# Stick-breaking attention: work taken off GpSimd, and the sum over later key blocks taken as separate products

## The chip, the cores and the metric

The kernel runs on one core of a Trainium2 chip. The metric is the device time of one execution in microseconds, the median of several runs. The engines are named as the profile names them: PE is TensorE (its weight loads are PEld), DVE is VectorE, ACT is ScalarE, POOL is GpSimd, SP is SyncE. Each engine takes its instructions in the order in which the program holds them.

## The reference

A trunk of two layers over 528 tokens (16 meta tokens and 512 real ones) of width 1024: layer 0 mixes tokens by stick-breaking attention with 16 heads of 64, layer 1 by a gated recurrence; a squared-ReLU MLP of width 4096 follows each. The change lies in the attention:

```python
def _sb_block(q_blk, k, v, q_pos):
    t_len = k.shape[2]
    k_pos = jnp.arange(t_len)
    z = jnp.einsum('bhqd,bhkd->bhqk', q_blk, k).astype(jnp.float32) * (SB_HEAD_DIM ** -0.5)
    causal = k_pos[None, :] < q_pos[:, None]
    log_keep = jnp.where(causal, -jax.nn.softplus(z), 0.0)
    after = lax.cumsum(log_keep, axis=3, reverse=True) - log_keep
    w = jnp.where(causal, jnp.exp(jax.nn.log_sigmoid(z) + after), 0.0)
    return jnp.einsum('bhqk,bhkd->bhqd', w.astype(v.dtype), v)
...
        h = h + stick_breaking_mixer(hn, sb_w_qkv[j], sb_w_o[j])
...
        h = h + sq_relu_mlp(hn, mlp_w_up[i], mlp_w_down[i])
```

So a weight needs, for its query, the softplus of all later keys up to that query: a sum that runs backwards over the keys.

## The kernel before

Every float32 operand of a product is written as two halves, a rounded one and the rest (`split`, lines 56 to 61: ACT or DVE makes the rounded half `hi`, line 58 or 60, and DVE or POOL subtracts it, line 61), and a product of two numbers is three matmuls. `load_unit` (line 88) loads 128 x 1024 weights and splits them into `whi` and `wlo`; `v_load` does the same for the weights of v.

The work goes by pairs of heads (`heads`, eight calls, p from 0 to 7), and while a pair is worked on, PE also makes the queries, keys and values of the next (`make_qk`, `make_v`), and behind the last pair the output projection (`proj`, weights `wo`). Within a pair there are two heads (e) and four blocks t of 128 keys. Keys lie on the partitions, and queries along the free dimension, so block t has 288, 272, 400 or 512 columns for t of 3, 2, 1, 0. The blocks go from the last to the first, both heads each time. For each block:

- `do_z`: PE writes scores and mask into the PSUM tile z (four such tiles);
- `do_soft` (lines 411 to 419): three ACT activations and one DVE instruction make softplus in `sp`, and DVE splits it into `sh` (line 60) and `sl` (line 61);
- `do_s` (lines 421 to 442): PE subtracts from z the sums within the block (the triangle `ntri` times sh and sl), and for blocks 2, 1 and 0 the sum over the later blocks, by products with `nones`, a matrix of -1. Block 2 takes sh and sl of block 3 as they are. For blocks 1 and 0, DVE has added softplus of the later blocks column by column into `sp` (lines 434 and 442); this running sum is split anew into `rh` and `rl` (line 438), and these are what `nones` multiplies;
- `do_o`: ACT takes exp of z, the weights are split into `wh` and `wl` (line 448; for blocks 3, 2, 1 by ACT and POOL, for block 0 by DVE), and PE multiplies with v.

POOL also makes the lower halves of the key weights (line 288), of half of the v weights (line 340), of wo (lines 563 and 585), of two half units at the start (line 217), and a small addition per head (line 478). The order on each engine is set by a scheduler, which places instructions by its own estimate of their durations; `tc.high_priority` moves some forward. An engine waits on semaphores for what it reads and for buffers to come free; temporary tiles have rings: 7 for sp, 4 each for sh and sl, 2 each for rh and rl.

Of the kernel before, what the change touches and what calls it, by code (L numbers as in the profile page):

```python
# [16 lines left out]
ALU = mybir.AluOpType  # L17
# [3 lines left out]
KC = 8  # L21
NM = 16
S = 512
T = NM + S
# [13 lines left out]
W3, W2, W1 = 320, 272, 400  # L38
# [3 lines left out]
def tile_hybrid_trunk(ctx: ExitStack, tc: tile.TileContext, h0, vec, wqk, wv, wo, wob,  # L42
# [13 lines left out]
    def split(src, hi, lo, hi_eng=None, lo_eng=None):  # L56
        if hi_eng is None or hi_eng is act:
            act.activation(out=hi, in_=src, func=AF.Copy)  # L58
        else:
            hi_eng.tensor_copy(out=hi, in_=src)  # L60
        (lo_eng or dve).tensor_tensor(out=lo, in0=src, in1=f32(hi), op=ALU.subtract)  # L61
# [26 lines left out]
    def load_unit(src, lo_eng=None, hi_eng=None):  # L88
        with tc.high_priority(HP):
            raw = wp.tile([P, KC * P], F32, tag="raw", name="raw", bufs=3)  # L90
            nc.sync.dma_start(out=raw, in_=src)
            hi = wp.tile([P, KC * P], F32R, tag="whi", name="whi")
            lo = wp.tile([P, KC * P], F32R, tag="wlo", name="wlo")
            split(raw, hi, lo, hi_eng, lo_eng)
        return hi, lo
# [73 lines left out]
    def attention_layer():  # L169
# [11 lines left out]
        def tmp(tag, bufs, dtype=F32):  # L181
            return ap_.tile([P, S], dtype, tag=tag, name=tag, bufs=bufs)
# [8 lines left out]
        def first_half(i, a, lo_eng=None):  # L191
            m, raw, hi, lo = w_first[i]
            half = slice(a * 4 * P, (a + 1) * 4 * P)
            nc.sync.dma_start(out=raw[:, half], in_=wqk[m][:, half])
            split(raw[:, half], hi[:, half], lo[:, half], None, lo_eng)
# [14 lines left out]
        for c in range(KC):  # L210
            if c % 4 == 0:
                hs[c // 4] = hsp.tile([P, 4, TX], F32, tag="hs", name="hs")
                first_half(0, c // 4)
            nc.sync.dma_start(out=h_chunk(c), in_=h0[:, c, :])
            xs_write(c, h_chunk(c), V_MIX0, 0, TX)
            if c % 4 == 3:
                first_half(1, c // 4, pool)
        for c in range(KC):
            first_add(c)
        dve.tensor_tensor(out=nrm.acc, in0=nrm.acc, in1=acc2[:, 0, :], op=ALU.add)  # L220
# [11 lines left out]
            pool.affine_select(out=t, in_=t, pattern=[[step, t.shape[1]]], base=base,  # L232
                               channel_multiplier=mult, compare_op=op, fill=fill)

        scr = tmp("sp", 7)
        t_ = scr[:, 0:P]
        pool.memset(t_, 1.0)
        aff(t_, 0, 1, -1, ALU.is_equal, 0.0)
# [7 lines left out]
        pool.memset(t_, 0.0)  # L246
        aff(t_, NM, -1, 1, ALU.is_gt, NEG)
        pool.tensor_copy(out=m0, in_=t_)
        scr = tmp("sp", 7)
        t_ = scr[:, 0:W2]  # L250
        pool.memset(t_, 0.0)
        aff(t_, 0, -1, 1, ALU.is_gt, NEG)
        pool.tensor_copy(out=m2, in_=t_)
        scr = tmp("sp", 7)
        pool.memset(scr[:, 0:W3], 0.0)
        aff(scr[:, 0:256], -112, -1, 1, ALU.is_gt, NEG)
        aff(scr[:, 256:272], 112, -1, 1, ALU.is_gt, NEG)
# [27 lines left out]
        o = ap_.tile([P, KC, T], F32, name="o")  # L285

        def qk_mm(m, new):
            hi, lo = load_unit(wqk[m], lo_eng=dve if m < KC else pool)
            gs = []
            for c0, n in ALL:  # L290
                g = new()
                gemm([g[:, 0:n]], [(c0, n)],
                     [(hi[:, k * P:(k + 1) * P], lo[:, k * P:(k + 1) * P], xh[k], xl[k]) for k in range(KC)])
                gs.append(g)
            return gs
# [37 lines left out]
        def v_load(g, lo_eng=None):  # L333
            vhi = hsp.tile([P, KC, 256], F32R, tag="hs", name="vhi")
            vlo = hsp.tile([P, KC, 256], F32R, tag="hs", name="vlo")
            for j in range(2):
                raw = wp.tile([P, KC * P], F32, tag="raw", name="raw", bufs=3)
                nc.sync.dma_start(out=raw, in_=wv[g, j])
                r3 = raw.rearrange("p (k n) -> p k n", n=256)
                split(r3, vhi[:, 4 * j:4 * j + 4, :], vlo[:, 4 * j:4 * j + 4, :], lo_eng=lo_eng or (pool, dve)[j])  # L340
            return vhi, vlo

        def v_mm(pv, w, vhi, vlo):
# [27 lines left out]
        def heads(p, q, kk, v2):  # L371
# [34 lines left out]
            def two(src, w, htag, ltag, bufs, hi_eng, lo_eng):  # L406
                h_, l_ = tmp(htag, bufs, F32R), tmp(ltag, bufs, F32R)
                split(src[:, 0:w], h_[:, 0:w], l_[:, 0:w], hi_eng, lo_eng)
                return h_, l_

            def do_soft(t, e):
                w, zt = width[t], z[t, e]
                a = sp[t, e] = tmp("sp", 7)
                act.activation(out=a[:, 0:w], in_=zt[:, 0:w], func=AF.Abs)  # L414
                table(out=a[:, 0:w], in_=a[:, 0:w], func=AF.Exp, tset=LNEXP, scale=-1.0)
                table(out=a[:, 0:w], in_=a[:, 0:w], func=AF.Ln, tset=LNEXP, bias=1.0)
                dve.scalar_tensor_tensor(out=a[:, 0:w], in0=zt[:, 0:w], scalar=0.0, in1=a[:, 0:w],  # L417
                                         op0=ALU.max, op1=ALU.add)
                sh[t, e], sl[t, e] = two(a, w, "sh", "sl", 4, dve, dve)

            def do_s(t, e):
                w, zt = width[t], z[t, e]
                for x in (sh[t, e], sl[t, e]):
                    mm(zt[:, 0:w], ntri, x[:, 0:w], False, False)
                if t == 3:
                    mm(zt[:, 240:256], ones, sp[t, e][:, 272:288], False, False)
                    a, h_, l_ = (x[3, e][:, 240:256] for x in (sp, sh, sl))
                    dve.tensor_tensor(out=a, in0=a, in1=sp[3, e][:, 272:288], op=ALU.add)
                    split(a, h_, l_, dve, dve)
                elif t == 2:  # L430
                    for x in (sh[3, e], sl[3, e]):
                        mm(zt[:, 16:W2], nones, x[:, 0:256], False, False)
                    r, r3 = sp[2, e], sp[3, e]
                    dve.tensor_tensor(out=r[:, 16:W2], in0=r[:, 16:W2], in1=r3[:, 0:256], op=ALU.add)
                else:
                    c = 128 if t == 1 else 112
                    wr = width[t + 1]
                    for x in two(sp[t + 1, e], wr, "rh", "rl", 2, dve if t else act, dve):
                        mm(zt[:, c:c + wr], nones, x[:, 0:wr], False, False)
                    if t == 1:  # L440
                        r = sp[1, e]
                        dve.tensor_tensor(out=r[:, 128:W1], in0=r[:, 128:W1], in1=sp[2, e][:, 0:W2], op=ALU.add)

            def do_o(t, e):
                w, zt = width[t], z[t, e]
                x = tmp("x", 2)
                table(out=x[:, 0:w], in_=zt[:, 0:w], func=AF.Exp, tset=LNEXP)
                ws = two(x, w, "wh", "wl", 2, act if t else dve, pool if t else dve)
                if t == 3:
                    for i, x in enumerate(ws):  # L450
                        mm(po[e][:, 256:512], vst(3, e), x[:, 0:256], i == 0, False)
                    for x in ws:
                        mm(zt[:, 288:320], vst(4, e), x[:, 256:288], False, False)
                    own, oth = sides[e]
                    m = ap_.tile([P, 2 * NM], F32, tag="om", name="om", bufs=2)
                    act.activation(out=m[own, :], in_=zt[oth, 288:320], func=AF.Copy)
                    dve.tensor_tensor(out=ends(o[own, p, :], NM), in0=zt[own, 288:320].rearrange("p (a b) -> p a b", a=2),
                                      in1=m[own, :].rearrange("p (a b) -> p a b", a=2), op=ALU.add)
                else:
                    c = {2: 240, 1: 112, 0: 0}[t]  # L460
                    for x in ws:
                        mm(po[e][:, c:c + w], vst(t, e), x[:, 0:w], False, False)
# [10 lines left out]
            for a, b in ((0, S),) if p < KC - 1 else ((0, HT - NM), (HT - NM, S)):  # L473
                for e, (own, oth) in enumerate(sides):
                    m = tmp("x", 2)
                    act.activation(out=m[own, a:b], in_=po[e][oth, a:b], func=AF.Copy)
                    if b == S:
                        pool.tensor_tensor(out=m[own, S - NM:], in0=o[own, p, T - NM:], in1=m[own, S - NM:], op=ALU.add)
                    dve.tensor_tensor(out=o[own, p, NM + a:NM + b], in0=po[e][own, a:b], in1=m[own, a:b], op=ALU.add)  # L479

        def decay():
# [78 lines left out]
            return xr  # L560

        for m in range(NA):
            proj(m, [(k, k) for k in range(6)], residual(m), load_unit(wo[m], lo_eng=pool))
        o_split(6)
        o_split(7, ALL)
        raw = wp.tile([P, KC * P], F32, tag="raw", name="raw", bufs=3)
# [14 lines left out]
        for m in (4, 5, 0, 1, 6, 2, 3, 7):  # L581
            if m < NA:
                proj(m, [(2 * m, 6), (2 * m + 1, 7)], h_chunk(m), wl_)
            else:
                proj(m, [(k, k) for k in range(8)], residual(m), load_unit(wo[m], lo_eng=pool), ztile)
            final(m)
        xs["h"], xs["l"] = xh, xl
        return nrm
# [316 lines left out]
```

## Time and profile before

| | |
|---|---|
| median of 3 runs | 1246.43 us (1243.47 to 1246.81) |
| the profiled execution | 1246.97 us; its span, from first to last instruction, 1245.1 us |
| PE busy | 1203.9 us, 97% of the span |
| DVE busy | 703.7 us, 57% |
| ACT busy | 562.1 us, 45% |
| POOL busy | 120.3 us, 10% |
| mean granted clock of PE | 0.989 |

The attention, with its output projection, takes about the first 345 us; the first MLP follows. Shares of the whole span are a mean over stages with different limits, so the stretch in which the change lies has to be read by itself. The profile's "busy" of PE counts a matmul from its start to its modelled end, and matmuls overlap, so PE can seem busy across a short pause. Granted clock 1.00 is the full 2.4 GHz; 0.5 would be 1.2 GHz.

### The profile page before, as it was taken

To read this page: it belongs to the slowest core of one execution; us is meant where nothing else is said; L and a number is where in the kernel's file an instruction comes from. 1 tells how busy PE (TensorE), PEld (TensorE's weight loads), DVE (VectorE), ACT (ScalarE), POOL (GpSimd) and SP (SyncE) were. 2 spreads that over 40 slices of the span, in tenths; PEclk is the share of its full clock that TensorE was granted. 3 is DMA by queue.
4 is the path that set the end of the run, shared out by engine and by line. 5 is a ranking of instruction groups with operands and counts; after the bars stand their busy time and mean duration, and the time that the engine had idled before them with its cause. 6 is when DMAs were issued, how large, how long until landed. Compare 5 with 4: busy or idle time off the path is not lost.

```text
span 1245.1 us, 19073 instructions
## 1 busy us (share of the span) xinstructions
PE 1203.9 (97%) x7836; PEld 1103.7 (89%) x7836; DVE 703.7 (57%) x1117; ACT 562.1 (45%) x943; POOL 120.3 (10%) x117
## 2 busy tenths in 40 slices
PE   7999999989999999999999999999999999999997
PEld 6999999878999999999999999777888888888886
DVE  6898989898654422244433377686644233444333
ACT  5777777776443321133322348664433221333321
POOL 5232332344100000000000000000000000000000
PEclk8999999998999999999999999999999999999998
DMA  6221303023222222322222331223233232332322
GB/s 209 81 92 35 90 32 104 18 84 106 69 83 88 85 97 74 102 94 94 85 92 79 102 119 54 83 85 102 87 100 102 85 102 87 100 101 85 102 85 68
DMA packets 33334, 110.13 MB, mean 88 GB/s; under 512 B 3936, under 2 KB 5984, under 8 KB 33248
## 3 DMA queue, kind: packets, MB, share of 16 engines
q1 hardware_dynamic: 32816, 108.53, 26.9%
q8 instruction: 61, 1.00, 0.3%
q10 hardware_dynamic: 432, 0.39, 0.1%
q14 instruction: 25, 0.20, 0.1%
HBM read 102.49 MB, written 2.10 MB: 84 GB/s over the span
## 4 chain that ended last, share of the span: by engine, by line
PE 77%; DVE 13%; ACT 6%; issue 3%; DMA 1%; POOL 0%; SPq 0%; DVEq 0%; ACTq 0%; POOLq 0%
PE g L98 72%; PE z L98 5%; DVE sl L61 2%; PE o L98 1%; DVE sh L60 1%; ACT sp L79 1%; ACT whi L58 1%; DVE k L322 1%; DVE wlo L61 1%; DVE sp L417 1%; DVE o L479 1%; ACT sp L414 1%; DVE th L723 1%; DVE rl L61 1%; DVE q L313 1%
## 5 line engine op out<-in xcount | busy, mean ns | idle before, releaser
L58 ACT ACTIVATE whi<-raw 128x1024 fp32r<-128x1024 f32 (+1 forms) x178 | 186.6, 1050 | 541.7 <-PE g L98 286.9
L61 DVE TENSOR_TENSOR wlo<-raw,whi 128x1024 fp32r<-128x1024 f32 (+1 forms) x161 | 196.7, 1222 | 253.2 <-PE g L98 131.7
L98 PE MATMUL g<-xl,whi 128*128 128x264 f32 (+1 forms) x720 | 231.9, 335 | 0.7 <-DVE xl L61 0.5
L98 PE MATMUL g<-xh,whi 128*128 128x264 f32 (+1 forms) x720 | 232.0, 336 | 0.1
L98 PE MATMUL g<-hh,whi 128*128 128x264 f32 (+2 forms) x784 | 229.3, 318 | 0.0
L98 PE MATMUL g<-hl,whi 128*128 128x264 f32 (+2 forms) x784 | 229.2, 318 | 0.0
L98 PE MATMUL g<-xh,wlo 128*128 128x264 f32 (+1 forms) x720 | 157.5, 335 | 0.8 <-DVE wlo L61 0.8
L98 PEld LDWEIGHTS g<-hl,whi 128*128 128x128 f32 x784 | 147.5, 188 | 11.2
L98 PEld LDWEIGHTS g<-hh,whi 128*128 128x128 f32 x784 | 147.6, 188 | 10.8
L98 PEld LDWEIGHTS g<-xl,whi 128*128 128x128 f32 x720 | 136.3, 189 | 15.8 <-DVE xl L61 1.6
L98 PEld LDWEIGHTS g<-xh,whi 128*128 128x128 f32 x720 | 136.3, 189 | 14.8 <-ACT r L79 0.3
L613 DVE SCALAR_TENSOR_TENSOR t<-g,rstd 128x264 f32<-128x264 f32 (+1 forms) x96 | 46.8, 516 | 172.4 <-PE g L98 172.3
L98 PE MATMUL g<-x,whi 128*128 128x264 f32 x1024 | 137.5, 284 | 1.8 <-DVE hs L553 1.8
L98 PE MATMUL g<-hh,wlo 128*128 128x264 f32 (+2 forms) x784 | 136.7, 319 | 0.0
L98 PEld LDWEIGHTS g<-x,whi 128*128 128x128 f32 x1024 | 130.7, 188 | 2.1 <-ACT whi L58 2.0
L98 PEld LDWEIGHTS g<-xh,wlo 128*128 128x128 f32 x720 | 118.7, 189 | 14.9 <-DVE wlo L61 1.1
L98 PEld LDWEIGHTS g<-hh,wlo 128*128 128x128 f32 x784 | 115.5, 188 | 10.8
L98 PE MATMUL g<-x,wlo 128*128 128x264 f32 x512 | 78.3, 285 | 0.0
L98 PEld LDWEIGHTS g<-x,wlo 128*128 128x128 f32 x512 | 69.2, 188 | 0.1
L79 ACT ACTIVATE sp<-sp 128x400 f32<-128x400 f32 (+3 forms) x128 | 62.0, 510 | 1.1
L61 POOL TENSOR_TENSOR wl<-x,wh 128x288 fp32r<-128x288 f32 (+2 forms) x48 | 53.1, 1113 | 70.6 <-ACT wh L58 48.1
L797 POOL MEMSET identf<- 128x128 f32 x1 | 0.2, 205 | 544.0 <-PE g L98 544.0
(201 smaller groups left out, 1779.6 us busy)
## 6 DMA issues: line engine op xcount, KB each, us to landing
raw<-in_wup_dram SPq DMA_DIRECT2D x64, 512.0 KB, 3.2
raw<-in_wdn_dram SPq DMA_DIRECT2D x64, 512.0 KB, 3.2
raw<-in_win_dram SPq DMA_DIRECT2D x16, 512.0 KB, 3.3
raw<-in_wqk_dram SPq DMA_DIRECT2D x14, 512.0 KB, 3.3
q<-q SPq DMA_DIRECT2D x16, 264.0 KB, 3.7
raw<-in_wv_dram SPq DMA_DIRECT2D x8, 512.0 KB, 3.3
raw<-in_wo_dram SPq DMA_DIRECT2D x8, 512.0 KB, 3.4
raw<-in_wout_dram SPq DMA_DIRECT2D x8, 512.0 KB, 3.3
```

Source lines behind the costliest of these rows:

```text
L58: act.activation(out=hi, in_=src, func=AF.Copy)
L60: hi_eng.tensor_copy(out=hi, in_=src)
L61: (lo_eng or dve).tensor_tensor(out=lo, in0=src, in1=f32(hi), op=ALU.subtract)
L79: ins = act.activation(out=out, in_=in_, func=func, **kw)
L98: return pe.matmul(out=o, lhsT=lhsT, rhs=rhs, start=start, stop=stop, skip_group_check=True)
L313: dve.tensor_tensor(out=q[own, e, 1, :], in0=t[own, 0:T], in1=f32(q[own, e, 0, :]), op=ALU.subtract)
L322: dve.tensor_tensor(out=kk[oth, e, :], in0=t[own, :], in1=f32(kk[own, e, :]), op=ALU.subtract)
L414: act.activation(out=a[:, 0:w], in_=zt[:, 0:w], func=AF.Abs)
L417: dve.scalar_tensor_tensor(out=a[:, 0:w], in0=zt[:, 0:w], scalar=0.0, in1=a[:, 0:w], op0=ALU.max, op1=ALU.add)
L479: dve.tensor_tensor(out=o[own, p, NM + a:NM + b], in0=po[e][own, a:b], in1=m[own, a:b], op=ALU.add)
L613: dve.scalar_tensor_tensor(out=t3[:, i, :], in0=g[:, i, 0:cw], scalar=0.0, in1=r3[:, i, :], op0=ALU.max, op1=ALU.mult)
L723: dve.tensor_tensor_scan(out=ths[n], data0=rs[n], data1=is_[n], initial=0.0, op0=ALU.mult, op1=ALU.add)
```

## The change

Block t now multiplies `nones` with the halves sh and sl of each later block by itself, so for block 1 four products and for block 0 six, where each had two. The running sum is gone: the two DVE additions and the splits into rh and rl. The halves of all four blocks have to live until block 0 is done, so their rings grow from 4 to 7, and that of sp shrinks to 5. Everything that POOL split or added in this stage is done by DVE. The masks and constants that POOL makes at the start, its three multiplications and additions for the first norm, and its few instructions at the very end of the program stay.

```diff
@@ first units, key weights, v weights
-                first_half(1, c // 4, pool)
+                first_half(1, c // 4)
...
-            hi, lo = load_unit(wqk[m], lo_eng=dve if m < KC else pool)
+            hi, lo = load_unit(wqk[m], lo_eng=dve)
...
-                split(r3, vhi[:, 4 * j:4 * j + 4, :], vlo[:, 4 * j:4 * j + 4, :], lo_eng=lo_eng or (pool, dve)[j])
+                split(r3, vhi[:, 4 * j:4 * j + 4, :], vlo[:, 4 * j:4 * j + 4, :], lo_eng=dve)
@@ do_soft, do_s, do_o
-                a = sp[t, e] = tmp("sp", 7)
+                a = sp[t, e] = tmp("sp", 5)
...
-                sh[t, e], sl[t, e] = two(a, w, "sh", "sl", 4, dve, dve)
+                sh[t, e], sl[t, e] = two(a, w, "sh", "sl", 7, dve, dve)
...
-                elif t == 2:
-                    for x in (sh[3, e], sl[3, e]):
-                        mm(zt[:, 16:W2], nones, x[:, 0:256], False, False)
-                    r, r3 = sp[2, e], sp[3, e]
-                    dve.tensor_tensor(out=r[:, 16:W2], in0=r[:, 16:W2], in1=r3[:, 0:256], op=ALU.add)
-                else:
-                    c = 128 if t == 1 else 112
-                    wr = width[t + 1]
-                    for x in two(sp[t + 1, e], wr, "rh", "rl", 2, dve if t else act, dve):
+                first = (NM, 128, 256, 272)
+                for t2 in range(t + 1, 4):
+                    c, wr = first[t2] - first[t], 256 if t2 == 3 else width[t2]
+                    for x in (sh[t2, e], sl[t2, e]):
                         mm(zt[:, c:c + wr], nones, x[:, 0:wr], False, False)
-                    if t == 1:
-                        r = sp[1, e]
-                        dve.tensor_tensor(out=r[:, 128:W1], in0=r[:, 128:W1], in1=sp[2, e][:, 0:W2], op=ALU.add)
...
-                ws = two(x, w, "wh", "wl", 2, act if t else dve, pool if t else dve)
+                ws = two(x, w, "wh", "wl", 2, act if t else dve, dve)
...
-                        pool.tensor_tensor(out=m[own, S - NM:], in0=o[own, p, T - NM:], in1=m[own, S - NM:], op=ALU.add)
+                        dve.tensor_tensor(out=m[own, S - NM:], in0=o[own, p, T - NM:], in1=m[own, S - NM:], op=ALU.add)
@@ output projection, twice
-            proj(m, [(k, k) for k in range(6)], residual(m), load_unit(wo[m], lo_eng=pool))
+            proj(m, [(k, k) for k in range(6)], residual(m), load_unit(wo[m]))
```

The scheduler reorders with it. The first place is DVE at the end of the third pair of heads, before. sp_1614 and sp_1639 are softplus of block 0 of the two heads, sp_1825 is block 3 of the next pair.

```order
L417 SCALAR_TENSOR_TENSOR sp_1639<-z_1558,sp_1639 128x512 [waits Activation_49]
L61 TENSOR_TENSOR rl_1651<-sp_1588,rh_1650 128x400 [waits Activation_49]
L61 TENSOR_TENSOR sl_1620<-sp_1614,sh_1619 128x512 [waits DVE_49]
L60 CAST sh_1644<-sp_1639 128x512 [waits DVE_49]
L302 SCALAR_TENSOR_TENSOR qk32_2107<-g_2082,rstd_437 128x264 [waits PE_49]
L61 TENSOR_TENSOR wlo_2622<-raw_2619,whi_2621 128x1024 [waits DMAHW1_49,Activation_49]
L61 TENSOR_TENSOR sl_1645<-sp_1639,sh_1644 128x512 [waits DVE_49]
L313 TENSOR_TENSOR q_2110<-qk32_2107,q_2110 64x528 [waits DMAHW6_49,DMAHW5_49,Activation_49]
L313 TENSOR_TENSOR q_2110<-qk32_2107,q_2110 64x528 [waits Activation_49]
L417 SCALAR_TENSOR_TENSOR sp_1825<-z_1805,sp_1825 128x288 [waits PE_49,Activation_49]
L60 CAST wh_1633<-x_1631 128x512 [waits Activation_49]
```

The same place in the changed kernel (block 0 is sp_1590 and sp_1615, the next pair's block 3 is sp_1801):

```order
L60 CAST sh_1595<-sp_1590 128x512 [waits DVE_49]
L417 SCALAR_TENSOR_TENSOR sp_1615<-z_1540,sp_1615 128x512 [waits Activation_49]
L61 TENSOR_TENSOR sl_1596<-sp_1590,sh_1595 128x512 [waits DVE_49]
L302 SCALAR_TENSOR_TENSOR qk32_2075<-g_2050,rstd_437 128x264 [waits PE_49]
L61 TENSOR_TENSOR wlo_2582<-raw_2579,whi_2581 128x1024 [waits DMAHW1_49,Activation_49]
L417 SCALAR_TENSOR_TENSOR sp_1801<-z_1781,sp_1801 128x288 [waits Activation_49]
L313 TENSOR_TENSOR q_2078<-qk32_2075,q_2078 64x528 [waits DMAHW6_49,DMAHW5_49,Activation_49]
L60 CAST sh_1620<-sp_1615 128x512 [waits PE_49]
L313 TENSOR_TENSOR q_2078<-qk32_2075,q_2078 64x528 [waits Activation_49]
L61 TENSOR_TENSOR sl_1621<-sp_1615,sh_1620 128x512 [waits DVE_49,PE_49]
L61 TENSOR_TENSOR wl_1585<-x_1582,wh_1584 128x400 [waits Activation_49]
L60 CAST sh_1806<-sp_1801 128x288 [waits PE_49]
```

rl is gone and a wl that POOL had made stands among the rows. The cast of the second head's block 0 (sh_1620), and that of the next pair's block 3 (sh_1806), now wait for PE: with rings of seven, the eighth tile takes the place of one that the products of block 0 read last. Between sl_1621 and sh_1806 stands one wl of 400 columns.

The second place is PE, block 0 of the first head of the same pair, before:

```order
L98 MATMUL o0_1424<-wl_1583,v2_1278 128x400 [waits Pool_49]
L98 MATMUL z_1532<-sl_1620,ntri_176 128x512 [waits DVE_49]
L98 MATMUL z_1532<-rh_1625,nones_177 128x400
L98 MATMUL z_1532<-rl_1626,nones_177 128x400
L98 MATMUL z_1558<-sh_1644,ntri_176 128x512 [waits DVE_49]
```

and in the changed kernel, as far as the next row of the projection (g):

```order
L98 MATMUL z_1515<-sl_1596,ntri_176 128x512 [waits DVE_49]
L98 MATMUL z_1515<-sh_1549,nones_177 128x400
L98 MATMUL z_1515<-sl_1550,nones_177 128x400
L98 MATMUL z_1515<-sh_1499,nones_177 128x272
L98 MATMUL z_1515<-sl_1500,nones_177 128x272
L98 MATMUL z_1515<-sh_1435,nones_177 128x256
L98 MATMUL z_1515<-sl_1436,nones_177 128x256
L98 MATMUL g_2091<-xh5_77,wlo_2088 128x264
```

Six products with nones follow the triangle where there were two, and none of the six has a wait of its own.

## Rows read from the trace of the kernel before

**Rows 1.** Windows (us): busy PE, PEld, DVE, ACT, POOL (count), granted clock, DMA

```profile
25.00:275.00 250.00, 237.36 (x1773) 227.52 (x1772) 226.15 (x479) 186.98 (x417) 83.34 (x67) 1.00 0.23 70
275.00:300.00 25.00, 25.00 (x168) 24.43 (x169) 18.97 (x45) 16.22 (x37) 8.89 (x8) 0.87 0.29 88
300.00:325.00 25.00, 21.55 (x128) 19.68 (x127) 16.31 (x27) 10.21 (x21) 5.30 (x5) 0.86 0.22 73
375.00:400.00 25.00, 25.00 (x207) 25.00 (x207) 11.86 (x19) 10.16 (x15) 0.00 (x0) 1.00 0.26 85
```

**Rows 2.** Waits on PE, 25 to 345 us: us in total, times, longest us

```profile
PE z L98 <- DVE sl L61: 4.9, 4, 2.0
PE z L98 <- DVE k L322: 3.7, 2, 3.4
PE z L98 <- DVE sh L60: 3.2, 5, 1.3
```

**Rows 3.** Groups by form, 0 to 480 us: busy us, mean ns, idle before

```profile
L60 DVE CAST sh<-sp 128x16 fp32r<-128x16 f32 x16 | 8.7, 542 | 0.2 <-PE z L98 0.2
L60 DVE CAST sh<-sp 128x512 fp32r<-128x512 f32 x16 | 11.3, 709 | 0.0
L60 DVE CAST wh<-x 128x512 fp32r<-128x512 f32 x16 | 6.7, 422 | 5.7 <-ACT x L79 5.5
L61 DVE TENSOR_TENSOR sl<-sp,sh 128x512 fp32r<-128x512 f32 x16 | 15.5, 975 | 0.1
L61 DVE TENSOR_TENSOR wl<-x,wh 128x512 fp32r<-128x512 f32 x16 | 11.0, 687 | 1.2 <-PE o L98 0.5
L322 DVE TENSOR_TENSOR k<-qk,k 64x544 fp32r<-64x544 f32 x16 | 16.0, 1001 | 1.5 <-ACT k L321 1.0
```

**Rows 4.** Tiles sh and k on DVE: ns min/median/max, first and last start

```profile
L60 DVE CAST sh<-sp x80: 156/358/2498, 44.8 to 309.4; 128x288 fp32r<-128x288 f32 x16, 128x16 fp32r<-128x16 f32 x16, 128x272 fp32r<-128x272 f32 x16, 128x400 fp32r<-128x400 f32 x16
L322 DVE TENSOR_TENSOR k<-qk,k x16: 718/721/2746, 37.9 to 276.0; 64x544 fp32r<-64x544 f32 x16
```

**Rows 5.** Timelines of DVE, POOL and PE near 275 and 306 us: start, us

```profile
272.18 2.75 DVE L322 TENSOR_TENSOR k<-qk,k 64x544 fp32r<-64x544 f32 x1
271.68 2.67 POOL L61 TENSOR_TENSOR wlo<-raw,whi 128x1024 fp32r<-128x1024 f32 x1
274.98 1.03 PE L98 MATMUL z<-q,k 128*128 128x256 f32 x4 [3.42 <-DVE k L322]
277.76 0.42 PE L98 MATMUL g<-xh,whi 128*128 128x264 f32 x1
277.98 0.42 PE L98 MATMUL g<-xl,whi 128*128 128x264 f32 x1
305.87 0.70 PE L98 MATMUL z<-sl,ntri 128*128 128x400 f32 x1 [2.04 <-DVE sl L61]
```

**Rows 6.** Work that goes: tile rl (ns min/median/max), then groups by form

```profile
L61 DVE TENSOR_TENSOR rl<-sp,rh x32: 423/561/2012, 54.2 to 309.0; 128x272 fp32r<-128x272 f32 x16, 128x400 fp32r<-128x400 f32 x16
L60 DVE CAST rh<-sp 128x272 fp32r<-128x272 f32 x16 | 6.7, 418 | 0.2
L434 DVE TENSOR_TENSOR sp<-sp 128x256 f32<-128x256 f32 x16 | 8.2, 512 | 0.1
L442 DVE TENSOR_TENSOR sp<-sp 128x272 f32<-128x272 f32 x16 | 6.9, 435 | 0.1
```

**Rows 7.** Groups by form, 0 to 480 us: DVE prices for moved work

```profile
L61 DVE TENSOR_TENSOR wlo<-raw,whi 128x1024 fp32r<-128x1024 f32 x31 | 37.9, 1222 | 32.9 <-PE g L98 23.2 <-ACT whi L58 9.7
L61 DVE TENSOR_TENSOR sl<-sp,sh 128x288 fp32r<-128x288 f32 x16 | 7.2, 453 | 0.2
```

**Rows 8.** Timeline of PE: start, us, of products that follow each other

```profile
296.82 0.52 PE L98 MATMUL z<-q,k 128*128 128x400 f32 x2
297.18 0.28 PE L98 MATMUL z<-m,ident 128*128 128x256 f32 x1
297.30 0.29 PE L98 MATMUL o<-wl,v 128*128 128x272 f32 x1
```

More of the change, by code (lines that the diff above doesn't have):

```diff
@@ L233, in aff @@
                                channel_multiplier=mult, compare_op=op, fill=fill)
-        scr = tmp("sp", 7)
+        scr = tmp("sp", 5)
         t_ = scr[:, 0:P]
@@ L248, in attention_layer @@
         pool.tensor_copy(out=m0, in_=t_)
-        scr = tmp("sp", 7)
+        scr = tmp("sp", 5)
         t_ = scr[:, 0:W2]
@@ L253, in attention_layer @@
         pool.tensor_copy(out=m2, in_=t_)
-        scr = tmp("sp", 7)
+        scr = tmp("sp", 5)
         pool.memset(scr[:, 0:W3], 0.0)
@@ L584, in attention_layer @@
             else:
-                proj(m, [(k, k) for k in range(8)], residual(m), load_unit(wo[m], lo_eng=pool), ztile)
+                proj(m, [(k, k) for k in range(8)], residual(m), load_unit(wo[m]), ztile)
             final(m)
```

## Prediction

> **What bounds the kernel now.** I read the windows first, since the change touches only the first 345 us. In the stretch from 25 to 275 us, which holds nearly all of the heads, PE is busy 237 of 250 us and DVE 226 of 250, so 90% [rows 1]. Two in-order engines are both nearly full, and each waits for the other at times. In the pure matmul stretch at 375 us, PE does 207 products of 264 columns in 25 us, one per 0.121 us, and is never idle [rows 1]. That pace tells more than "busy". In the heads' stretch stand 1773 products. At 0.121 us each they need 214.5 us. The wide ones cost more: two of 400 columns take 0.36 us together, so 0.18 each, while products of 256 and 272 columns follow each other at 0.12 [rows 8]; in proportion 512 columns cost 0.23. A head has eight of 400 and six of 512, and the stretch holds about 14 heads: 14 x (8 x 0.06 + 6 x 0.11) = 16 us. Six narrow ones per head, taken at nothing, take 10 us off. That leaves 220 of 250 us; some records can be missing, so I put PE's lost time there at 25 us.
>
> Who ends it shows in the list of waits on PE: DVE's sl, k and sh, 11.8 us together [rows 2]. These are plain short instructions, so the next question is why they come late. The groups by form answer it. Casting 128x512 costs DVE 709 ns for sh and 422 for wh; the subtraction of the same shape costs 975 for sl and 687 for wl; a cast of 16 columns costs 542 [rows 3], though the shortest sh takes 156; k takes 1001 on average, but 718 at least and 2746 at most [rows 3, 4]. So some executions are stretched severalfold. The timeline shows one: POOL's wlo runs from 271.68 for 2.67 us; DVE's k begins in it, at 272.18, and ends 0.6 us after it; PE waits 3.42 us for k, and then issues products every 0.22 us instead of 0.12 [rows 5]: it has fallen from its 2.4 GHz level to 1.2. The granted clock is 0.87 and 0.86 in the two windows from 275 to 325 us [rows 1]; in the second, too, a wait for DVE stands, 2.04 us for sl at 305.87 [rows 5]. The Trainium skill (SBUF — State Buffer, "Who interferes with whom") has a rule for this: GpSimd and DVE share one pair of ports, and the later of the two is blocked for the whole instruction of the other. By it k would last 274.35 - 272.18 + 0.72 = 2.89 us; the trace says 2.75, so it agrees.
>
> **The change, part by part.**
>
> *PE gains work.* Block 1 has two more products of 256 columns, block 0 two of 272 and two of 256: six per head, 96 in 16 heads, at 0.12 us [rows 8]: **+11.6 us**. PE is the engine that is nearly full and nothing covers this, except time in which PE would have waited anyway.
>
> *DVE loses work.* Per head the two additions (512 and 435 ns), the cast to rh (418) and two subtractions to rl (561 at the median) go: 2.49 us, times 16, 39.8 us [rows 6]. ACT loses the other cast to rh.
>
> *DVE gains POOL's work.* 7 key units, 8 units of wo and 3 of v at 1.22 us make 22.0; two half units some 1.3; wl of 288 columns at 0.45, of 272 at no more than that, and of 400 at 0.57 (between 453 ns for 288 and 687 for 512), 16 times each, 23.5; 16 additions on 16 columns at 0.16, 2.6 [rows 3, 4, 7]. Together +49.4 us.
>
> *DVE is no longer stretched.* From four forms alone, 16 of each: (542 - 156) + (709 - 422) + (975 - 687) + (1001 - 718) ns, times 16, is 19.9 us [rows 3, 4]; other forms come on top. So DVE ends with 49.4 - 39.8 - 19.9, **10 us less work** or better, although it took over what POOL did. Bounds: 10 us more, if the stretching has another cause; 30 less, if all other forms together gain as much again as these four. None of this is on the path by itself. It counts where PE waits for DVE.
>
> *PE's lost time in the heads.* Of 25 us I let half go: **-12.5**. That is the listed waits for the three DVE results, without the 2.04 at 306 (9.8 us, [rows 2, 5]), and a small part of the short ones that no row names. Bounds: only the wait for k goes (-3.4); all 25 go. I take the middle because the stretched forms are just those named in the waits, while the new order brings waits of its own.
>
> *PE's lost time in the tail.* The clock: 25 x 0.13 + 25 x 0.14 = 6.75 us in two windows [rows 1]; with the wait at 306, **-8.8**. PE sat idle before both falls, in waits for k and for sl. If neither wait is there, I expect the clock to stay up. Bounds: 0 (another wait takes their place) and -8.8.
>
> *The start.* Two half units move from POOL to DVE, while POOL's multiplications for the norm stay and go on colliding. 1.3 us more on DVE, less stretching: 0, within 1.5 either way.
>
> *Rings.* Softplus halves now live through the whole pair, and the casts of the second head's block 0 and of the next pair's block 3 wait for PE to read the tile whose place they take. What stands behind them on DVE is wl and wh for block 0 and evictions of the next projection. Eight products of block 0 last 2 x (0.23 + 0.18 + 0.12 + 0.12) = 1.3 us; the wl between takes 0.57, so such a cast can wait 0.7 us and more. I take 0 for it, since DVE has room for it now; its upper bound is in the rivals. Buffers of sp (5 in place of 7) cost nothing, as sp is done once its halves exist.
>
> *Sum:* 11.6 - 12.5 - 8.8 = -9.7 us. From the profiled 1246.97 that gives 1237.3; the median of the runs shown is 0.5 us lower, so I predict **1236.7 us**. (No change means within 0.3%, or 3.7 us: about what a measurement of this kernel can tell.)
>
> **Rivals.**
>
> *Deep gain.* All of PE's lost time goes, 25 in the heads and 8.8 in the tail: 11.6 - 33.8 = -22, about 1224 us. For it: DVE has more room everywhere, and the chain between blocks is shorter, because block 0 needs no addition, cast and subtraction on the way. Against it: short waits arise in any such interleaving.
>
> *A wash.* The gain is only the wait for k and the tail, 12.2 us, and the 96 products take back 11.6: 1246 us. For it: PE was 95% busy in the heads, and work added to a full engine is certain, while work off its partner is not.
>
> *Slower, by the rings.* Two casts per pair wait for PE up to 1.3 us each, 15 of them in eight pairs, and all that DVE owes PE stands behind them: 15 x 1.3 = 20 us handed on to PE, so 1236.7 + 20 = 1257. It decides the sign from 9.7 / 15 = 0.65 us per wait that reaches PE. Against it: products of the next projection lie between, which PE does meanwhile.
>
> *Slower, by load.* If the stretching isn't POOL's doing, DVE, at 90% before, gets 49.4 - 39.8 = 10 us more and hands it on to PE, which has 11.6 more of its own: up to 1268 if both add, 1257 if one hides the other. The rows speak against it, as above. The Trainium skill (Perfetto Trace Analysis, "Optimizing Scalar/DVE Operations") has a rule against this change: work of a saturated DVE may go to another engine, even GpSimd. It adds that between these two it might not help, for the shared port; rows 5 bear out the addition.
>
> *The change is not what it says.* POOL keeps the masks, the norm and the end, all outside the heads, so in the heads it really is idle; I give this no chance.
>
> **How the numbers follow.** Forecast (-4 to -17 us) 0.61, deep gain 0.16, wash 0.13, slower by the rings 0.06, by load 0.04. Faster by over 0.3% are the first two, 0.77; same 0.13; slower 0.10. The range runs from 1222, just beyond the deep gain's middle, to 1249, which takes in the wash with room for 2 or 3 us of the new waits; outside it I leave about 0.07 below and 0.12 above.
>
> **What would show it.** POOL has no row between 25 and 345 us. Mean durations of sh, sl and k are at their free values: 512 columns at 0.42 and 0.69, k at 0.72. DVE's busy time from 25 to 345 us falls by at least 10 us. 96 more products with nones. The granted clock stays near 1.00 around 300 us. DVE waits for PE before a cast to sh, 15 or so times. The first MLP begins about 10 us earlier. I am wrong if sh and sl stay stretched without POOL (load), if DVE's waits for PE at sh come up again as waits of PE (rings), or if the tail still has its waits and low clock (wash).

## The result, and the profile after

The changed kernel takes 1231.47 us (median of 4 runs, 1231.26 to 1233.84), the kernel before 1245.74 beside it (4 runs, 1243.47 to 1246.81). The ratio is 0.9892, with a 95% interval from 0.9873 to 0.9911: 14.3 us faster. Forecast were 9.7 us less and 1236.7, and the time lies inside the range of 1222 to 1249. The profiled execution is the slowest of the four, 1233.84 us with a span of 1231.9.

The windows of the changed kernel, in the columns of [rows 1]:

```profile
12.00:25.00 13.00, 12.67 (x103) 12.45 (x101) 11.27 (x12) 6.67 (x10) 4.41 (x3) 1.00 0.50 169
25.00:275.00 250.00, 247.30 (x1890) 242.67 (x1889) 206.67 (x494) 190.35 (x418) 0.00 (x0) 0.99 0.24 74
275.00:300.00 25.00, 22.32 (x149) 20.94 (x148) 20.08 (x45) 16.52 (x35) 0.00 (x0) 0.93 0.34 105
300.00:325.00 25.00, 25.00 (x202) 24.67 (x201) 17.64 (x35) 12.86 (x22) 0.00 (x0) 1.00 0.25 79
```

POOL has no row from 25 to 345 us. From 25 to 275 us PE does 1890 products where it did 1773, and DVE is busy 207 us where it was 226, although it also does what POOL did. One fall of the clock is left, to 0.93 in the window from 275, and the one after 300 is gone. The one that is left stands behind three waits of PE for DVE's wb, sh and sl, 1.20, 0.85 and 0.63 us long, which end between 290 and 293 us.

The groups by form of the changed kernel, DVE, 0 to 480 us, answer [rows 3] and the first of [rows 7]:

```profile
L61 DVE TENSOR_TENSOR wlo<-raw,whi 128x1024 fp32r<-128x1024 f32 x48 | 58.7, 1222 | 44.9 <-PE g L98 31.2 <-ACT whi L58 13.7
L322 DVE TENSOR_TENSOR k<-qk,k 64x544 fp32r<-64x544 f32 x16 | 11.5, 720 | 0.5
L61 DVE TENSOR_TENSOR sl<-sp,sh 128x512 fp32r<-128x512 f32 x16 | 11.0, 685 | 2.6 <-PE z L98 2.5
L60 DVE CAST sh<-sp 128x512 fp32r<-128x512 f32 x16 | 6.7, 420 | 2.0 <-PE z L98 2.0
L60 DVE CAST sh<-sp 128x16 fp32r<-128x16 f32 x16 | 2.6, 167 | 2.5 <-PE z L98 2.5
```

The forms that were stretched have their free durations: sl 685 ns for 975, sh 420 for 709, k 720 for 1001. The tile k on DVE shows that no execution is stretched any more, where the longest in [rows 4] took 2746 ns:

```profile
L322 DVE TENSOR_TENSOR k<-qk,k x16: 718/721/722, 35.7 to 265.5; 64x544 fp32r<-64x544 f32 x16
```

The waits on PE from 25 to 345 us, as [rows 2]. The 11.8 us for sl, k and sh are now 1.8:

```profile
PE z L98 <- DMA q<-q: 1.9, 2, 1.7
PE g L98 <- DVE wb L61: 1.2, 1, 1.2
PE z L98 <- DVE sl L61: 1.0, 2, 0.6
PE z L98 <- DVE sh L60: 0.8, 1, 0.8
```

Where the time came from is read from three products that both programs have. They are the first of the v projection, the last pair's mask product of 320 columns, and the first of the MLP. PE's timeline before (start, us; in brackets idle time and releaser):

```profile
27.31 0.28 PE L98 MATMUL g<-vhi,xh 128*128 128x256 f32 x1
...
268.35 0.31 PE L98 MATMUL z<-m,ident 128*128 128x320 f32 x1
...
344.38 0.60 PE L98 MATMUL g<-x,whi 128*128 128x264 f32 x3 [1.83 <-DVE hs L553]
```

and of the changed kernel:

```profile
22.23 0.28 PE L98 MATMUL g<-vhi,xh 128*128 128x256 f32 x1
...
261.98 0.31 PE L98 MATMUL z<-m,ident 128*128 128x320 f32 x1
...
329.64 0.60 PE L98 MATMUL g<-x,whi 128*128 128x264 f32 x3 [0.82 <-DVE hs L545]
```

The changed kernel is ahead by 5.1 us at the first of them, by 6.4 at the second, and by 14.7 at the third. So the start gave 5.1, the heads 1.3 and the tail 8.4. Behind that it loses 1.5 of 900 us, which leaves the 13.2 us between the two spans. Of the 96 added products 75 stand between the first two places, and 21 between the second and the third. The three leads are distances in one trace of each kernel; whether a lead at the start is kept or lost on the way is a question of its own, which the experiments on the start take up.

### The profile page after: what moved, and what is told of

It is laid out like the page before. It is cut to its first block, busy times and chain, and to the rows that moved or that the text cites. A ratio compares the mean times of both kernels' runs of the same rounds, so it can differ in the third digit from the quotient of the medians.

```text
span 1231.9 us, 19086 instructions
## 1 busy us (share of the span) xinstructions
PE 1205.1 (98%) x7932; PEld 1110.6 (90%) x7932; DVE 672.6 (55%) x1121; ACT 558.4 (45%) x927; POOL 15.5 (1%) x33
## 4 chain that ended last, share of the span: by engine, by line
PE 90%; DVE 5%; ACT 3%; issue 2%; DMA 1%; SPq 0%; DVEq 0%; ACTq 0%
PE g L98 79%; PE z L98 9%; PE o L98 2%; DVE wlo L61 1%; ACT whi L58 1%; DVE th L715 1%; ACT r L79 0%; DVE i L714 0%; DMA hs<-in_h_dram 0%; DVE xl L129 0%; ACT th L79 0%; DVE y L749 0%; DMA q<-q 0%; ACT L79 0%; DVE rstd L159 0%
## 5 line engine op out<-in xcount | busy, mean ns | idle before, releaser
L61 DVE TENSOR_TENSOR wlo<-raw,whi 128x1024 fp32r<-128x1024 f32 (+1 forms) x178 | 215.6, 1212 | 257.2 <-PE g L98 131.8
L79 ACT ACTIVATE sp<-sp 128x288 f32<-128x288 f32 (+3 forms) x128 | 62.2, 510 | 1.3
L98 PE MATMUL g<-vhi,xl 128*128 128x256 f32 x160 | 46.1, 289 | 0.0
L98 PE MATMUL g<-vhi,xh 128*128 128x256 f32 x160 | 46.1, 288 | 0.0
```

The lines of the kernel that those rows point to most:

```text
L79: ins = act.activation(out=out, in_=in_, func=func, **kw)
L98: return pe.matmul(out=o, lhsT=lhsT, rhs=rhs, start=start, stop=stop, skip_group_check=True)
```

## Experiments

**The two halves of the change, each alone.** The first keeps POOL's work and takes the products:

```diff
@@ against the kernel before
-                a = sp[t, e] = tmp("sp", 7)
+                a = sp[t, e] = tmp("sp", 5)
-                sh[t, e], sl[t, e] = two(a, w, "sh", "sl", 4, dve, dve)
+                sh[t, e], sl[t, e] = two(a, w, "sh", "sl", 7, dve, dve)
...
-                    for x in two(sp[t + 1, e], wr, "rh", "rl", 2, dve if t else act, dve):
+                for t2 in range(t + 1, 4):
+                    c, wr = first[t2] - first[t], 256 if t2 == 3 else width[t2]
+                    for x in (sh[t2, e], sl[t2, e]):
...
```

> The kernel before with only the products changed: separate products with nones from each later block's halves, rings of 7 and 5, and all work of POOL left where it was. Port theory (POOL's reads of SBUF stretch DVE, and the gain comes from taking them away): the means of sh and sl for 512 columns stay near 0.71 and 0.97 us, PE gets 96 products or 11.6 us more, DVE about 40 us less; time between 1241 and 1256 us, so little or nothing of the gain of 13 us. Rival (the gain comes from DVE's load, that is from the running sum that goes): most of the gain is here, 1230 to 1237 us.

Measured: 1237.33 us, ratio 0.9935 (0.9922 to 0.9948), 8.5 us faster. That is less than the 1241 to 1256 of the one theory and just above the 1230 to 1237 of the other, so neither holds alone. Its windows:

```profile
12.00:25.00 13.00, 10.19 (x82) 9.73 (x80) 12.27 (x12) 6.43 (x9) 5.62 (x4) 1.00 0.46 145
25.00:275.00 250.00, 244.77 (x1856) 238.68 (x1856) 197.73 (x419) 187.53 (x412) 79.06 (x67) 0.99 0.24 73
```

DVE has 28 us less to do than before, and PE does 83 products more in the same 250 us. The stretching stays: k takes 1203 ns on average and the 512-column sl 853. Not all of the gain is the products' doing: of the 9.6 us between the two spans, 3.4 stand at the first product of v already (23.89 for 27.31 us), where the granted clock is 1.00 from 12 to 25 us and was 0.76 before, though the edit takes no work off the start.

The second, called the moves alone below, has all that takes work off POOL, and keeps the running sum:

```diff
@@ against the changed kernel
-                a = sp[t, e] = tmp("sp", 5)
+                a = sp[t, e] = tmp("sp", 7)
-                sh[t, e], sl[t, e] = two(a, w, "sh", "sl", 7, dve, dve)
+                sh[t, e], sl[t, e] = two(a, w, "sh", "sl", 4, dve, dve)
...
-                for t2 in range(t + 1, 4):
...
+                    for x in two(sp[t + 1, e], wr, "rh", "rl", 2, dve if t else act, dve):
...
```

> The changed kernel with the running sum of before (additions, rh and rl, rings of before): only POOL's work is moved to DVE. Port theory: sh, sl and k at their free values (0.42, 0.69, 0.72 us), no added products on PE; DVE gains 49 us of work and loses some 50 of stretching, so it is as full as before, but no longer late by jumps; 1229 to 1239 us. Rival (DVE's load): DVE gets 49 us more in a stage where it was 90% busy, so slower than before by 5 to 15 us, 1251 to 1261.

Measured: **1225.13 us**, ratio 0.9833 (0.9819 to 0.9846), 20.7 us faster than before, and 6.3 faster than the changed kernel, which is more than either theory expected. Its first product of v starts at 22.25 us, as early as in the changed kernel. Its window:

```profile
25.00:275.00 250.00, 245.67 (x1877) 240.06 (x1875) 233.15 (x578) 200.62 (x437) 0.00 (x0) 1.00 0.26 79
```

DVE is busy for more of the stretch than before, 233 us against 226, and PE is late less. So DVE's share of busy time did not tell how often PE would wait for it. With the free durations (k at 720 ns, sl at 688) 578 instructions fit where 479 did. This also decides the rival *by load*: work piled onto a DVE that was 90% busy, and the kernel became faster.

The two gains don't add: 8.5 and 20.7 apart, 14.3 together. The products gain 8.5 us while POOL works and cost 6.3 once it doesn't.

**Is it POOL's being busy, or its late results?** Both halves above could also work because wl and wlo came late from POOL. So POOL gets work that nobody reads, in both kernels:

```diff
@@ against the changed kernel, and against the moves alone
                 ws = two(x, w, "wh", "wl", 2, act if t else dve, dve)
+                if t:
+                    junk = tmp("junk", 1)
+                    pool.tensor_tensor(out=junk[:, 0:w], in0=x[:, 0:w], in1=x[:, 0:w], op=ALU.subtract)
+                    pool.tensor_tensor(out=junk[:, 0:w], in0=junk[:, 0:w], in1=junk[:, 0:w], op=ALU.subtract)
```

To make room for the unread tile, the ring of sp gets one buffer fewer than the kernel had, 4 in the changed kernel and 6 in the moves alone. The lighter load has one such subtraction a block, in the changed kernel alone.

> The changed kernel, and POOL does 48 subtractions that nobody uses: of x from itself, in the shapes and at the places where it made wl before (the ring of sp is 4 in place of 5 to make room for the tile). Nobody waits for their result; only the two tiles of x come free later. Port theory: sh and sl for 512 columns are stretched again (means above 0.5 and 0.75 us), single executions of sh over 1 us; time 1234 to 1243. Rival (DVE was late because it waited its turn for what POOL made, not for the port): sh and sl stay at 0.42 and 0.69, no single one over 0.45 and 0.75; time within 2 us of the changed kernel, 1230 to 1234.

Measured: 1232.45 us, ratio 0.9897 (0.988 to 0.9913), no difference from the changed kernel that can be told, so the time expected for a working POOL (1234 to 1243) was missed, and four buffers of sp cost nothing that can be told either. The window shows that the load itself worked:

```profile
25.00:275.00 250.00, 246.32 (x1891) 241.59 (x1890) 218.42 (x494) 190.53 (x418) 36.72 (x42) 1.00 0.24 73
```

The same 494 instructions keep DVE busy 218.42 us in place of 206.67, and the longest sh takes 1079 ns in place of 428, yet PE loses nothing. DVE has 31 us left in this stretch, and the stretching fits into it. So the load was doubled, and put on the kernel with the running sum too. First the changed kernel:

> The changed kernel (1231.5, VectorE busy 206.7 of 250 us in 25:275) with the same unused work on POOL, some 80 us of it in 25:275; one sp buffer fewer. Theory 'a working POOL stretches VectorE': some 25 us more of VectorE's busy time, to 232, which still fits in 250, so the time moves by 0 to +4 (1231 to 1236), much less than with the running sum: the products are worth something only where VectorE is stretched. Rival 'POOL's own late results': no change, and the same as with the running sum.

Measured: 1238.85 us, ratio 0.9944 (0.9932 to 0.9957), 7.4 us slower than the changed kernel, where 0 to 4 was expected. With the running sum and seven buffers of sp there is no room for the unread tile (the attention's tiles would need 86.5 kb per partition, and 85.1 are left), so this form, for which 1233 to 1243 had been expected, has no time. The moves alone with six buffers are the control for the last one:

> The control for the run with the running sum and the unused POOL work: the moves off POOL with the running sum and six sp buffers in place of seven, no unused work. Expected by both theories: 1224 to 1227, as with seven.

Measured: 1225.1 us, ratio 0.9831 (0.9818 to 0.9844); the buffer is worth nothing that can be told. And the same with the load:

> The moves off POOL with the running sum kept and six sp buffers (1225.1, VectorE busy 233 of 250 us in 25:275), and unused work on POOL: behind each split of x of blocks 3 to 1 two subtractions of the same size whose result nobody reads, the second on its own tile alone. The changed kernel with the same work came out at 1238.9, 7.4 us longer. Theory 'a working POOL stretches VectorE, and that was the price': VectorE has less room here (233 busy of 250, against 206.7), so the loss is larger than 7.4: 1236 to 1250, no longer better than the changed kernel under the same load. Rival 'what POOL cost before was its own late results (wl, wlo), not VectorE's pace': 7 us at most, as in the changed kernel, 1225 to 1232.

Measured: **1249.74 us**, ratio 1.0025 (1.0014 to 1.0035), 24.6 us slower than its control and not faster than the kernel before any more, by POOL instructions whose results go nowhere. It lies at the upper end of the 1236 to 1250 expected. The windows of the control and of this kernel:

```profile
25.00:275.00 250.00, 245.75 (x1868) 240.27 (x1867) 231.66 (x573) 199.25 (x434) 0.00 (x0) 0.99 0.26 79
```

```profile
25.00:275.00 250.00, 236.81 (x1722) 225.50 (x1721) 239.70 (x530) 182.98 (x404) 71.09 (x80) 0.98 0.23 70
```

Under the load DVE is busy longer and gets less done, 530 instructions for 573, and PE gets 146 products less far. The waits on PE from 25 to 345 us are those on DVE's products again:

```profile
PE o L98 <- DVE wl L61: 4.0, 5, 1.6
PE g L98 <- DVE xl L61: 3.5, 4, 1.6
PE z L98 <- DVE sh L60: 2.9, 4, 1.6
```

The timeline of DVE and POOL in this kernel shows single instructions (start, duration):

```profile
103.55 0.69 DVE L417 SCALAR_TENSOR_TENSOR sp<-z,sp 128x512 f32<-128x512 f32 x1
104.16 0.34 DVE L354 SCALAR_TENSOR_TENSOR v<-g,rtok,v 128x128 fp32r<-128x128 f32 x1
104.26 0.85 POOL L451 TENSOR_TENSOR junk<-x 128x400 f32<-128x400 f32 x1 [7.80 <-ACT x L79]
104.41 1.13 DVE L61 TENSOR_TENSOR rl<-sp,rh 128x400 fp32r<-128x400 f32 x1
105.19 1.06 POOL L452 TENSOR_TENSOR junk<-junk 128x400 f32<-128x400 f32 x1
105.47 1.07 DVE L60 CAST sh<-sp 128x512 fp32r<-128x512 f32 x1
106.33 0.92 POOL L451 TENSOR_TENSOR junk<-x 128x400 f32<-128x400 f32 x1
106.46 1.22 DVE L61 TENSOR_TENSOR rl<-sp,rh 128x400 fp32r<-128x400 f32 x1
...
109.61 0.56 DVE L61 TENSOR_TENSOR wl<-x,wh 128x400 fp32r<-128x400 f32 x1
```

Two rl of 400 columns take 1.13 and 1.22 us and a cast of 512 columns 1.07, each begun inside a POOL instruction. With POOL idle the same forms take 0.57 and 0.42, as the free wl of 400 columns at 109.61 shows too, with 0.56. The whole trace says the same: 12 of the 16 rl of 400 columns begin inside a POOL instruction and take 1.14 us on average, and the four that meet none take 0.56. Nothing waits for these POOL results but ACT, once, for 0.4 us in the other kernel. So POOL's being busy is enough for the loss. That late wl and wlo cost something besides is not excluded.

With the load the products are worth 0.8% (1.0025 less 0.9944, 10 us); without it they cost 6.3 us. Both loaded kernels start alike (first product of v at 22.09 and 22.49 us), so this difference owes nothing to the start. This is the interaction of the first two experiments once more.

**How many products pay.** The sum over blocks 3 and 2 is formed and split once, and blocks 1 and 0 both use it; block 0 adds the halves of block 1 as products. Per head that is two products more than before and four less than in the changed kernel:

```diff
@@ against the changed kernel
-                sh[t, e], sl[t, e] = two(a, w, "sh", "sl", 7, dve, dve)
+                sh[t, e], sl[t, e] = two(a, w, "sh", "sl", 5, dve, dve)
...
+                    dve.tensor_tensor(out=r[:, 16:W2], in0=r[:, 16:W2], in1=r3[:, 0:256], op=ALU.add)
+                    st["sum", e] = two(r, W2, "rh", "rl", 2, dve, dve)
...
-                for t2 in range(t + 1, 4):
+                    for t2 in range(t + 1, 3):
...
-                    for x in (sh[t2, e], sl[t2, e]):
+                        for x in st["sum", e] if t2 == 2 else (sh[t2, e], sl[t2, e]):
```

> Between the changed kernel and the one with POOL's work moved only: the sum of blocks 3 and 2 is formed and split once and serves blocks 1 and 0; block 1 comes into block 0 by its own halves. PE: 4 products for block 0 and 2 for block 1, so 2 of 272 columns more per head than with the full running sum (4 us in all), and 4 of 256 fewer than in the changed kernel (7.6 us). DVE: 18 us more than in the changed kernel, 16 less than with the full running sum. Theory that PE's columns alone count once POOL is idle: 1225.1 + 4 = 1229, or 1231.5 - 7.6 = 1224; so 1224 to 1229. Rival (DVE at 93% is a bound as well, and relief there pays): below 1224.

Measured: **1223.91 us**, ratio 0.9826 (0.9812 to 0.9841), 21.5 us faster than before and 7.6 faster than the changed kernel. It lies on the line between the two expectations, and does not decide between them. Its window:

```profile
25.00:275.00 250.00, 247.06 (x1889) 241.52 (x1888) 223.93 (x554) 194.02 (x425) 0.00 (x0) 1.00 0.25 77
```

The changed kernel has 64 products more: 7.56 / 64 = 0.118 us each, the full price of a narrow product, although it leaves DVE 17 us less busy (224 to 207). If they cost their full price, that relief bought nothing. Against the moves alone, this kernel has 32 products more (3.8 us at that price) and DVE is 9 us less busy (233 to 224), and the time is 1.2 us less, about as much as the runs spread: there, by the same price, the relief paid for the products. It beats the kernel before and the changed one; whether it beats the moves alone is not settled, since the two intervals overlap.

**The start.** The lower halves of the two half units go from POOL to DVE alone, in the kernel before, and go back to POOL in the changed kernel:

```diff
-                first_half(1, c // 4, pool)
+                first_half(1, c // 4)
```

> The kernel before with only the lower halves of the second unit's two halves at the start moved from POOL to DVE. In the changed kernel the first product with v came 5.1 us earlier (22.2 against 27.3 us). Theory that these two instructions did it (less time in which POOL reads beside DVE, and PE's clock not falling between 12 and 25 us): the first product with v near 22 us and the whole 3 to 5 us shorter, 1241 to 1243. Rival (the lead at the start is lost in the heads, which are bound by DVE): within 1.5 us of before. Second rival (the clock at the start changes from one execution to the next by itself): the first product with v near 27 us here, or anywhere between.

Measured: 1243.89 us (11 runs), ratio 0.9985 (0.9976 to 0.9995), 1.9 us faster than before, between the two expectations. In the profiled execution the start is that of the changed kernel: the first product of v at 22.26 us, and the clock at 1.00:

```profile
12.00:25.00 13.00, 12.61 (x102) 12.39 (x101) 11.30 (x12) 6.81 (x10) 4.44 (x3) 1.00 0.49 164
```

The lead of 5.1 us is still there at the first product of the MLP (339.26 for 344.38), and the span is 3.8 us shorter; the medians differ by less.

> The changed kernel with only these two instructions put back on POOL. Theory: the first product with v near 27 us again, and the whole 3 to 5 us longer than the changed kernel, 1235 to 1237. Rivals: within 1 us of the changed kernel.

Measured: 1232.55 us, ratio 0.9891 (0.9874 to 0.9909), 1.1 us above the changed kernel, within the spread. So these units are worth 1 to 2 us, while the trace shows a lead of 5.1 at the first product of v. The window from 12 to 25 us of the kernel before tells part of why:

```profile
12.00:25.00 13.00, 10.04 (x60) 9.41 (x60) 12.28 (x12) 7.63 (x11) 6.55 (x5) 0.76 0.41 124
```

and the same window with the half units back on POOL in the changed kernel:

```profile
12.00:25.00 13.00, 11.32 (x85) 10.90 (x83) 12.28 (x12) 6.95 (x10) 6.18 (x4) 1.00 0.43 139
```

The clock fell to 0.76 there only in the kernel before. Two kernels whose half units are on POOL as well keep 1.00: this one, and the products alone, whose window is shown above. Their first product of v starts at 24.4 and 23.9 us, against 27.3 before and 22.2 in the changed kernel. So in these traces some 3 of the 5.1 us go with that fall and 2 with the half units. And the 2 were not kept: with the half units back on POOL, the second of the three places stands at 261.83 us, level with the changed kernel's 261.98. Why these two kernels avoid the fall, and whether it is in every run of the kernel before, is open. PE's waits alone don't tell: up to 25 us the products alone have the same two waits for DVE's xl as the kernel before, 1.27 and 1.54 us, and keep 1.00.

A further step takes the norm's last POOL work off too (two multiplications and an addition), on top of the moves alone:

```diff
@@ against the moves alone
-            if c in (4, 7):
-                x, n = h_chunk(c), int(c == 7)
-                pool.tensor_tensor(out=acc2[:, n, :], in0=x, in1=x, op=ALU.mult)
...
-            else:
-                nrm.add(c, h_chunk(c))
+            nrm.add(c, h_chunk(c))
```

> The kernel with POOL's work moved and the running sum kept, and in addition POOL's three instructions for the first norm go (ACT squares and DVE adds these two chunks too). Then POOL does no more than masks before the heads. In the changed kernel three xl instructions took 4.95 us together beside these, where one takes 0.77. Theory that they delay the first products: the first product with v comes 1 to 3 us earlier than at 22.2 us, and the whole is 1 to 3 us shorter, 1222 to 1224. Rival (ACT and DVE get as much work as they are spared, or the first stage waits for the loads): 1224.5 to 1227.

Measured: 1228.37 us, ratio 0.986 (0.9845 to 0.9874): 3.2 us slower than the moves alone, and above both expectations. The first product of v comes 1.2 us earlier (21.0 for 22.2), but the MLP begins 1.8 us later (323.78 for 321.94). In the tail its clock is lower, 0.86 from 275 to 300 us where the moves alone have 0.93, and PE waits for wl:

```profile
PE o L98 <- DVE wl L61: 3.5, 3, 1.8
```

The order of the whole stage shifts with an edit at its start. What of the 3.2 us is due to that, and what to the work that ACT and DVE took over, was not separated.

**The rings.** The halves of each block get rings of their own (four tiles for block 3, two for the others) in place of one ring of seven:

```diff
@@ against the changed kernel
-                sh[t, e], sl[t, e] = two(a, w, "sh", "sl", 7, dve, dve)
+                sh[t, e], sl[t, e] = halves("sh", t), halves("sl", t)
+                split(a[:, 0:w], sh[t, e], sl[t, e], dve, dve)
```

> The changed kernel with sh and sl in rings of their own for each block, as wide as the block (four tiles for block 3, two each for 2, 1 and 0), so that no cast waits for PE to read another block's tile; the same work. In the changed kernel DVE waited 4.6 us for PE before casts to sh and 2.9 before subtractions to sl. Theory that these waits hold the changed kernel back: 1226 to 1229. Rival (DVE has time, and PE is full there): within 1.5 us of the changed kernel, 1230 to 1233.

Measured: 1231.65 us, ratio 0.989 (0.9876 to 0.9905), the same as the changed kernel. The waits on DVE from 25 to 345 us, of the changed kernel:

```profile
DVE sh L60 <- PE z L98: 4.6, 5, 1.5
...
DVE sl L61 <- PE z L98: 2.9, 4, 0.8
```

and with rings by block:

```profile
DVE sh L60 <- PE z L98: 1.8, 2, 1.5
...
DVE sl L61 <- PE z L98: 0.4, 1, 0.4
```

So 5.3 us of DVE's waits go and the time stays. DVE does wait for these buffers, but PE doesn't pay for it.

## Why the prediction was right, and where not

**What bounds the kernel** was read rightly: POOL's work stretches DVE's, PE waits, and its clock falls behind the waits. The load whose results nobody reads shows the cause, since it brings the loss back: 24.6 us.

**PE's lost time in the heads** (-12.5) was a little smaller. The heads are 1.3 us shorter although 75 of the added products stand in them, 9.0 us by the prediction's price, so 10.3 us of lost time went.

**The tail** (-8.8) was larger than its bound. It is 8.4 us shorter with the other 21 products in it, 2.5 us, so 10.9 us of lost time went. The clock was a part of it: the two windows gave up 0.13 and 0.14 of 25 us before, and 0.07 and nothing now, 5.0 us instead of the 6.75 forecast. The rest is waits: those listed on PE behind the second place fall from 9.7 us to 3.8. Heads and tail together, with the products, come to just the -9.7 of the sum; that they do so to the tenth, with the heads some 2 us under their term and the tail 2 us over, is luck.

**The start** (0, within 1.5) is the term that was mis-sized in the trace: it gave 5.1 us. The sum missed that the granted clock was 0.76 from 12 to 25 us; the windows were read from 25 us on. What it says of the half units alone was nearly right: 1 to 2 us. By the spans, the error of the sum, 13.2 against 9.7, is this term less the 1.5 lost behind the attention. How much of the 5.1 the change earned, and how much is a fall of the clock in the one profiled execution of the kernel before, stays open.

**DVE's balance** (10 us less work) came out just beyond its far bound: busy time over the whole program falls from 703.7 us to 672.6, by 31.1, where the bound was 30. Two things were mis-sized. The stretching was far more than the 19.9 us of four forms, as other forms have it too: rl up to 2012 ns [rows 6]. And the durations of neighbours overlap: sp at 103.55 lasts 0.69 us to 104.24, and the next one on DVE, 0.34 long, begins at 104.16. So a sum of durations overstates what moves or goes, here the 39.8 and the 49.4 alike: from the moves alone to the changed kernel, where the running sum goes and POOL is idle in both, DVE's busy time falls by 23.9 us (696.5 to 672.6). None of it was in the sum of the times.

**The added products** (+11.6) were priced rightly only where nothing else depends on them. At the margin, 64 of them cost 0.118 us each. But all 96 against the running sum cost 6.3 us, so by that price the sum's work on DVE still delayed PE by some 5 us even with POOL idle. The prediction kept both effects in one balance, and so did not see that the two halves of the change work against each other. Its *deep gain* (1224) was there to be had, by the moves alone or with a third of the products.

**The rivals.** *By the rings*: the waits came, nine for sh and sl together and 7.5 us long (five of them before a cast to sh, where 15 or so were expected), but not up to PE; rings that don't wait change nothing. *By load*: the moves alone decide against it, though DVE's load does count while POOL works, as the products under load show. *A wash*: against the trace, as both the heads' lost time and the tail gave more than the wait for k. The Trainium skill's suggestion to relieve a saturated DVE with another engine, even GpSimd (Perfetto Trace Analysis, "Optimizing Scalar/DVE Operations"), fails here by 20.7 us; its own doubt, that between these two it might not help, is what the runs bear out.

## What to carry to other kernels

An engine that is 90% busy may be so because a neighbour stretches its instructions. Compare the mean and the longest duration of a form with its shortest before taking work off it; here giving it the neighbour's work too made the kernel 20.7 us faster. Measure the parts of a change apart: a part that relieves a bound can be a cost once another part has removed it. Here a third of the products did no harm (1223.9 against 1225.1 us), and all of them cost 6.3 us.

## What was not expected

The load on POOL seems to have a point from which it tells. In the changed kernel 37 us of POOL work between 25 and 275 us cost nothing that can be told, and 75 us cost 7.4; with the running sum, 71 us cost 24.6. Nor is every form on DVE stretched. In the loaded kernel with the running sum, the instruction that reads z from PSUM (sp<-z,sp) is never longer than 692 ns (693 in the kernel before), while sl of the same 512 columns rises to 1339. POOL is busy at times when it runs: in the kernel before at least 11 of its 64 executions begin inside a POOL instruction, four of them with 512 columns, and these four take 0.68 us on average, as those that meet none do. Five sl of 512 columns that begin inside a POOL instruction take 1.45 us on average there, and nine that meet none 0.68. So POOL did not delay that form there; whether its operand in PSUM is the reason was not tried.
